# Group A's attention scores: keys without zero padding, two heads in the two row halves of the tensor engine

## The chip, the cores and the metric

The kernel runs on one core of one Trainium2 chip. A core has five engines that work from queues of their own, each in the order of its queue: TensorE (PE; its weight loads are listed as PEld), VectorE (DVE), ScalarE (ACT), GpSimd (POOL) and SyncE (SP, which here issues the loads). Matrix products read SBUF, the core's working memory of 128 partitions, and write PSUM, eight banks of 512 float32 columns on the same 128 partitions. The metric is device time in microseconds, lower is better.

## The reference

One decoder layer over 256 tokens of width 1024, in float32. Two groups of eight heads each attend side by side. Group A, which the change touches, has heads of 64:

```python
xn = rms_norm(h, norm_mix_g)
proj = jnp.einsum('bsd,de->bse', xn, w_in)
qa, ka, va, c_q, c_kv, k_rope = jnp.split(proj, cuts, axis=-1)
qa = rms_norm(qa.reshape(b, s, N_HEADS_A, HEAD_DIM_A), qnorm_a_g)
ka = rms_norm(ka.reshape(b, s, N_HEADS_A, HEAD_DIM_A), knorm_a_g)
...
out_a = dilated_attention(qa, ka, va, rel_bias).reshape(b, s, WIDTH_A)
...
mixed = jnp.concatenate([out_a, out_b], axis=-1)
h = h + jnp.einsum('bse,ed->bsd', mixed, w_o)
hn = rms_norm(h, norm_ffn_g)
hid = jnp.square(jax.nn.relu(jnp.einsum('bsd,df->bsf', hn, w_ff1)))
h = h + jnp.einsum('bsf,fd->bsd', hid, w_ff2)
```

dilated_attention is a causal softmax of q k / 8 plus a bias by distance, in which a key counts once for each of three dilated windows that reaches it. Group B is latent attention: its queries and keys come from the latents c_q and c_kv by a second projection.

## The kernel before

The 256 tokens are two tiles of 128. Large products run as three passes over operands that are split into a high and a low part (type float32r): ScalarE casts the high part (L215 for weights, L244 for activations), VectorE subtracts it (L216, L245). Weights come in chunks on the SP queue and are split piece by piece just ahead of their use. Small products (scores, mixed values, transposes) are plain float32.

Up to group B's attention the order of each queue is set by a scheduler, which interleaves the steps by its own estimate of their times; the order of the program and the number of buffers bound it. The steps of this part are: q and k of group A (projection, norm per head, transposition into qT_a and kT_a), group A's scores, the latents' projection (columns 384, 384 and 288 wide), group A's v (512 wide), the transposition and split of the latents (transposed_split: transposes of nats into a bank of the pool mm, then L244 and L245 into cT), and from there on group B's up-projections, first that of q (384 wide), for which an order is written out by hand.

qT_a holds a pair of heads on its 128 partitions: the even head on 0 to 63, the odd one on 64 to 127. kT_a has a block of 128 partitions for each head, filled with zeros by GpSimd (L344) and then with the head's keys in its own half (L378 on VectorE for the even heads, L379 on ScalarE for the odd ones). So the score product of a head contracts over all 128 partitions, and the other head's queries meet zeros.

UNITS divides the eight heads and two token tiles into six units of one PSUM bank each: for four heads at a time, the first tile's queries with 128 keys (four heads in a bank), and twice the second tile's queries with 256 keys (two heads in a bank). A unit goes through scores (PE into a bank of the pool sc, which has two), probs (VectorE adds the bias and finds the least, L402; ScalarE's exp, L405; VectorE's reciprocal and scaling, L406 and L408) and keys_first (four transposes into a bank of mm, which also has two, and a copy into pts, by VectorE for the first tile, L421, by ScalarE for the second, L423). Every matmul and transpose is issued on L144 or L147.

A function that the prediction reads as a pattern is values: it takes an even and an odd head in the two halves of the array's columns, 64 columns of weights each. In the trace these are the rows sc<-pts,va and mm<-pts,vb, with 128*64 as their rows and columns of the array.

## Time and profile before

| | |
|---|---|
| runs | 321.79, 322.65, 323.81 us; median 322.65 |
| profiled execution, span from first to last instruction | 320.9 us |
| PE busy, share of the span | 313.9 us, 98% |
| DVE, ACT, POOL busy | 204.9, 175.6, 38.4 us |
| granted TensorE clock, mean | 1.000 |

The profile gives the span of its execution alone; the runs' times hold what lies around a span as well. In a timeline a row begins with its start in microseconds from the span's begin and its length; neighbouring instructions of one kind are merged (x4). A matmul's length overlaps that of the next one, so the distance between starts tells what one costs in a stream. A plain float32 product shows as two records.

### The profile page before, as it was taken

To read this page: it belongs to the slowest core of one execution; us is meant where nothing else is said; L and a number is where in the kernel's file an instruction comes from. 1 tells how busy PE (TensorE), PEld (TensorE's weight loads), DVE (VectorE), ACT (ScalarE), POOL (GpSimd) and SP (SyncE) were. 2 spreads that over 40 slices of the span, in tenths; PEclk is the share of its full clock that TensorE was granted. 3 is DMA by queue.
4 is the path that set the end of the run, shared out by engine and by line. 5 is a ranking of instruction groups with operands and counts; after the bars stand their busy time and mean duration, and the time that the engine had idled before them with its cause. 6 is when DMAs were issued, how large, how long until landed. Compare 5 with 4: busy or idle time off the path is not lost.

```text
span 320.9 us, 4942 instructions
## 1 busy us (share of the span) xinstructions
PE 313.9 (98%) x1898; PEld 279.6 (87%) x1898; DVE 204.9 (64%) x384; ACT 175.6 (55%) x298; POOL 38.4 (12%) x61
## 2 busy tenths in 40 slices
PE   7999999999999999999999999999999999999995
PEld 4878999989986887899989989989889899899883
DVE  3769899955887993758774464654654745644632
ACT  5775568947785683448553553543633633535400
POOL 1025501180467000002000000000000000000000
PEclk9999999999999999999999999999999999999999
DMA  7989555153933263308655564646556564654002
GB/s 223 384 349 320 200 173 192 49 158 99 307 113 83 62 249 132 133 0 283 242 190 205 154 240 143 226 157 202 192 158 234 147 226 154 196 199 131 0 28 105
DMA packets 12296, 56.46 MB, mean 176 GB/s; under 512 B 1480, under 2 KB 3792, under 8 KB 7536
## 3 DMA queue, kind: packets, MB, share of 16 engines
q1 hardware_dynamic: 11072, 55.02, 50.3%
q10 hardware_dynamic: 1200, 1.12, 1.1%
q8 instruction: 15, 0.25, 0.3%
q14 instruction: 9, 0.07, 0.1%
HBM read 55.07 MB, written 1.06 MB: 175 GB/s over the span
## 4 chain that ended last, share of the span: by engine, by line
PE 96%; DMA 1%; ACT 1%; DVE 0%; issue 0%; DVEq 0%; SPq 0%; ACTq 0%
PE acc L144 58%; PE sc L144 19%; PE mm L144 15%; PE mm L147 4%; DMA big<-in_xt_dram 1%; ACT big L573 0%; ACT sqs L356 0%; ACT big L244 0%; ACT nats L593 0%; DVE x L706 0%; DVEq L759 0%; SPq L205 0%; ACT vb L597 0%; ACTq L244 0%
## 5 line engine op out<-in xcount | busy, mean ns | idle before, releaser
L144 PE MATMUL acc<-his,big 128*128 128x512 f32 (+2 forms) x576 | 176.2, 381 | 1.2 <-ACT big L244 1.2
L216 DVE TENSOR_TENSOR los<-raw,his 128x1024 fp32r<-128x1024 f32 (+3 forms) x106 | 121.5, 1149 | 85.9 <-ACT his L215 85.6
L215 ACT CAST his<-raw 128x1024 fp32r<-128x1024 f32 (+3 forms) x106 | 104.4, 992 | 100.5 <-PE acc L144 41.6
L144 PEld LDWEIGHTS acc<-his,big 128*128 128x128 f32 x576 | 107.4, 190 | 19.0 <-ACT big L244 1.9
L144 PE MATMUL acc<-los,big 128*128 128x512 f32 (+2 forms) x288 | 109.3, 380 | 0.0
L144 PEld LDWEIGHTS acc<-los,big 128*128 128x128 f32 x288 | 54.7, 190 | 8.6 <-issue 0.6
L144 PE MATMUL sc<-big,his 128*128 128x256 f32 x256 | 46.3, 283 | 0.0
L144 PE MATMUL mm<-big,his 128*128 128x256 f32 x256 | 46.2, 283 | 0.0
L144 PEld LDWEIGHTS sc<-big,his 128*128 128x128 f32 x256 | 40.2, 192 | 0.3
L144 PEld LDWEIGHTS mm<-big,his 128*128 128x128 f32 x256 | 40.1, 192 | 0.2
L144 PE MATMUL mm<-big,los 128*128 128x256 f32 x128 | 36.1, 283 | 0.0
L144 PE MATMUL sc<-big,los 128*128 128x256 f32 x128 | 36.0, 284 | 0.0
L144 PEld LDWEIGHTS mm<-big,los 128*128 128x128 f32 x128 | 24.5, 192 | 0.0
L144 PEld LDWEIGHTS sc<-big,los 128*128 128x128 f32 x128 | 24.5, 192 | 0.0
L405 ACT ACTIVATE half<-half,mx 128x128 f32<-128x128 f32 (+1 forms) x32 | 14.2, 445 | 4.4 <-DVE mx L402 4.2
L681 DVE TENSOR_TENSOR half<-half 128x512 f32<-128x512 f32 x16 | 10.9, 684 | 0.0
L684 DVE TENSOR_TENSOR big<-half,big 128x512 fp32r<-128x512 f32 x16 | 10.9, 684 | 0.0
L245 DVE SCALAR_TENSOR_TENSOR big<-mm,cols,big 128x256 fp32r<-128x256 f32 x16 | 7.3, 481 | 5.5 <-ACT big L244 5.2
L244 ACT ACTIVATE big<-mm,cols 128x256 fp32r<-128x256 f32 x16 | 7.3, 475 | 6.0 <-PE mm L147 5.8
L147 PE MATMUL mm<-ident,half 128*128 128x128 f32 x64 | 9.9, 273 | 0.0
L683 ACT CAST big<-half 128x512 fp32r<-128x512 f32 x16 | 9.7, 613 | 0.0
L147 PEld LDWEIGHTS mm<-ident,half 128*128 128x128 f32 x64 | 7.9, 140 | 1.5 <-DVE half L408 0.2
(129 smaller groups left out, 221.2 us busy)
## 6 DMA issues: line engine op xcount, KB each, us to landing
raw<-in_weights_dram SPq DMA_DIRECT2D x37, 1024.0 KB, 4.8
raw<-in_weights_dram SPq DMA_DIRECT2D x10, 512.0 KB, 3.6
raw<-in_weights_dram SPq DMA_DIRECT2D x6, 768.0 KB, 4.6
raw<-in_weights_dram SPq DMA_DIRECT2D x2, 576.0 KB, 4.1
raw<-in_weights_dram SPq DMA_DIRECT2D x4, 256.0 KB, 5.2
big<-in_xt_dram SPq DMA_DIRECT2D x4, 256.0 KB, 5.3
x<-in_x_dram SPq DMA_DIRECT2D x2, 512.0 KB, 8.5
big<-vec_d ACTq DMA_DIRECT2D x1, 1024.0 KB, 6.9
```

The costliest lines, as they stand in the source:

```text
L144: return self._issue(self.tc.nc.tensor.matmul(**kw))
L147: return self._issue(self.tc.nc.tensor.transpose(**kw))
L215: A.copy(out=hi, in_=raw)
L216: V.tensor_tensor(out=lo, in0=raw, in1=hi.bitcast(F32), op=ALU.subtract)
L244: a = A.activation(out=hi, in_=src, func=AF.Copy, scale=g)
L245: v = V.scalar_tensor_tensor(out=lo, in0=src, scalar=g, in1=hi.bitcast(F32), op0=ALU.mult, op1=ALU.subtract)
L405: A.activation(out=sb[:, i, :], in_=sb[:, i, :], func=AF.Exp, scale=-1.0, bias=mx[:, i:i + 1], accum_out=mx[:, 4 + i:5 + i])
L681: V.tensor_tensor(out=s2, in0=z, in1=z, op=ALU.mult)
L683: A.copy(out=ht[:, sl, :], in_=s3)
L684: V.tensor_tensor(out=ht[:, 4 + 2 * b:6 + 2 * b, :], in0=s3, in1=ht[:, sl, :].bitcast(F32), op=ALU.subtract)
```

## The change

kT_a becomes a tile of the shape of qT_a: a pair of heads on 128 partitions, no zeros and no fill, and one copy on VectorE in place of two. scores_a issues, for four heads and one token tile, four products of 64 rows each: the even head on partitions 0 to 63, the odd one on 64 to 127, in turn, the even heads into one bank and the odd ones into another. The bank is then a unit of two heads with every second head, so there are eight units; those of the first tile fill 256 columns of their bank, and have two transposes. probs and keys_first follow the unit's size. (The new file has its comments taken out, and its lines are numbered otherwise.)

```diff
-    kT_a = big.tile([P, H, S], F32, name="big")
-    G.memset(kT_a, 0.0)
+    kT_a = keep.tile([P, H // 2, S], F32, name="kT_a")
...
             else:
-                kv = kT_a.rearrange("p (h two) s -> p h two s", two=2)
-                V.tensor_copy(out=kv[0:64, :, 0, ts], in_=t3[0:64])
-                A.copy(out=kv[64:128, :, 1, ts], in_=t3[64:128])
...
+                V.tensor_copy(out=kT_a[:, :, ts], in_=t3)
...
-        sb = halft().rearrange("p (h k) -> p h k", h=n)
+        sb = halft(n * nk).rearrange("p (h k) -> p h k", h=n)
...
+        n, nk = sb.shape[1:]
+        blocks = n * nk // P
         flat = sb.rearrange("p h k -> p (h k)")
         ps = bank()
-        for i in range(4):
+        for i in range(blocks):
             T.transpose(out=ps[:, i * P:(i + 1) * P], in_=flat[:, i * P:(i + 1) * P], identity=ident)
         i = hs[0] - h0
+        dst = pT[:, i:i + (n - 1) * hs.step + 1:hs.step]
+        ps = ps[:, :blocks * P]
         if t == 0:
-            V.tensor_copy(out=pT[:, :, 0, :], in_=ps.rearrange("p (h s) -> p h s", h=4))
+            V.tensor_copy(out=dst[:, :, 0, :], in_=ps.rearrange("p (h s) -> p h s", h=n))
         else:
-            A.copy(out=pT[:, i:i + 2, 1:3, :], in_=ps.rearrange("p (h k s) -> p h k s", h=2, k=2))
+            A.copy(out=dst[:, :, 1:3, :], in_=ps.rearrange("p (h k s) -> p h k s", h=n, k=2))
...
-    for u in UNITS:
-        ps = scores(u, lambda h: qT_a[:, h // 2, :], lambda h: kT_a[:, h, :])
-        keys_first(u, probs(u, ps, lambda h: bias_r[:, h, ::-1], lambda t, h: -1.0), pT_a[u[0]])
...
+    def scores_a(h0):
...
+        for t in range(NT):
+            nk = (t + 1) * P
+            ps = [bank(sc).rearrange("p (h k) -> p h k", k=nk) for _ in range(2)]
+            for i in range(2):
+                for o in range(2):
+                    rs = slice(o * DA, (o + 1) * DA)
+                    T.matmul(out=ps[o][:, i, :], lhsT=qT_a[rs, h0 // 2 + i, t * P:(t + 1) * P], rhs=kT_a[rs, h0 // 2 + i, 0:nk], start=True, stop=True)
+            for o in range(2):
+                yield (h0, t, range(h0 + o, h0 + 4, 2)), ps[o][:, 0:2, :]
+
+    for h0 in (0, 4):
+        for u, ps in scores_a(h0):
+            keys_first(u, probs(u, ps, lambda h: bias_r[:, h, ::-1], lambda t, h: -1.0), pT_a[h0])
```

The scheduler orders the queues anew. On TensorE, the scores of the first four heads and the first tile stood like this, sc_396 being their one bank, with products of the latents' projection (acc) between them:

```order
L144 MATMUL sc_396<-big_207,qT_a_213 128x128
L144 MATMUL acc_618<-his_637,big_123 128x384
L144 MATMUL acc_618<-los_638,big_123 128x384
L144 MATMUL acc_618<-his_637,big_124 128x384
L144 MATMUL acc_617<-his_655,big_123 128x384
L144 MATMUL sc_396<-big_207,qT_a_213 128x128 x3
```

They stand like this now, sc_393 being the bank of the even heads and sc_394 that of the odd ones:

```order
L144 MATMUL acc_626<-his_646,big_124 128x384
L144 MATMUL sc_393<-kT_a_207,qT_a_212 128x128
L144 MATMUL sc_394<-kT_a_207,qT_a_212 128x128
L144 MATMUL sc_393<-kT_a_207,qT_a_212 128x128
L144 MATMUL sc_394<-kT_a_207,qT_a_212 128x128
```

The four products are together now, and the halves take turns; the same four heads' products of 256 columns stand in one such run of four a little later.

The scores of heads 4 to 7 are on TensorE further on. For the first tile sc_461 is the bank of the even heads and sc_462 that of the odd ones:

```order
L144 MATMUL acc_717<-his_736,big_124 128x288
L144 MATMUL sc_461<-kT_a_207,qT_a_212 128x128 x2
L144 MATMUL acc_716<-his_736,big_123 128x288
L144 MATMUL acc_716<-los_737,big_123 128x288
L144 MATMUL sc_462<-kT_a_207,qT_a_212 128x128 x2
L144 MATMUL acc_716<-his_736,big_124 128x288
```

For the second tile, sc_493 is the bank of the even heads and sc_494 that of the odd ones, and the transposes are those of two earlier units:

```order
L144 MATMUL acc_717<-his_770,big_123 128x288
L144 MATMUL sc_493<-kT_a_207,qT_a_212 128x256
L147 MATMUL mm_440<-ident_111,half_431 128x128 x4
L147 MATMUL mm_455<-ident_111,half_446 128x128 x4
L144 MATMUL sc_493<-kT_a_207,qT_a_212 128x256
L144 MATMUL sc_494<-kT_a_207,qT_a_212 128x256 x2
L144 MATMUL acc_717<-los_771,big_123 128x288
```

Here the products of one half stand together, apart from those of the other half, save for the second and third of the second tile.

On ScalarE, around the copies of group A's v out of its banks (va), the order was this; L423 copies the last two units' transposed probabilities, L244 makes the high parts of the transposed latents:

```order
L423 COPY pts<-mm 128x2x256
L215 CAST his<-raw 128x768
L423 COPY pts<-mm 128x2x256
L244 ACTIVATE big<-mm,cols 128x256
L215 CAST his<-raw 128x768
L244 ACTIVATE big<-mm,cols 128x256
L557 ACTIVATE va_209<-acc,rstd 128x512
L557 ACTIVATE va_210<-acc,rstd 128x512
L215 CAST his<-raw 128x768
L244 ACTIVATE big<-mm,cols 128x256 x2
```

It is this now, with L424 for L423 and L572 for L557:

```order
L424 COPY pts<-mm 128x2x256
L215 CAST his<-raw 128x768
L424 COPY pts<-mm 128x2x256
L572 ACTIVATE va_208<-acc,rstd 128x512
L572 ACTIVATE va_209<-acc,rstd 128x512
L215 CAST his<-raw 128x768
L244 ACTIVATE big<-mm,cols 128x256 x6
L215 CAST his<-raw 128x768
```

The two L244 that stood ahead of the copies of v are behind them and behind a cast. VectorE's L245 stand in a row of six in the same way, behind the low part of that cast. On TensorE the transposes of these latents, which were four ahead of v's last products and two behind them, are six behind them:

```order
L144 MATMUL acc<-his,big 128x512
L147 MATMUL mm<-ident,nats 128x128 x6
L144 MATMUL acc<-his,big 128x384
L144 MATMUL acc<-los,big 128x384
L144 MATMUL acc<-his,big 128x384 x2
```

## Rows read from the trace of the kernel before

**Rows 1.** The page: busy time (part 1) and chain of waits (part 4).

```profile
PE 313.9 (98%) x1898; PEld 279.6 (87%) x1898; DVE 204.9 (64%) x384; ACT 175.6 (55%) x298; POOL 38.4 (12%) x61
...
PE 96%; DMA 1%; ACT 1%; DVE 0%; issue 0%; DVEq 0%; SPq 0%; ACTq 0%
```

**Rows 2.** Busy time by stretch: us, PE, PEld, DVE, ACT, POOL, then PEclk, DMA.

```profile
40.00:50.00 10.00, 10.00 (x64) 9.86 (x63) 9.11 (x40) 6.74 (x20) 0.00 (x0) 1.00 0.64 214
50.00:60.00 10.00, 10.00 (x71) 9.66 (x70) 9.74 (x36) 8.67 (x26) 1.48 (x4) 1.00 0.30 99
```

**Rows 3.** Timeline of PE, 51.2 to 54.2 us: start, length, what.

```profile
51.45 1.69 PE L144 MATMUL sc<-big,qT_a 128*128 128x256 f32 x10
52.98 0.60 PE L147 MATMUL mm<-ident,half 128*128 128x128 f32 x4
53.42 0.39 PE L144 MATMUL sc<-big,qT_a 128*128 128x128 f32 x2
```

**Rows 4.** Timeline of PE, 124.2 to 126.5 us, at group B's mixed values.

```profile
124.04 0.39 PE L144 MATMUL acc<-los,big 128*128 128x512 f32 x1
124.26 0.40 PE L144 MATMUL acc<-his,big 128*128 128x512 f32 x1
124.59 1.52 PE L144 MATMUL mm<-pts,vb 128*64 128x256 f32 x16
126.04 0.50 PE L144 MATMUL acc<-his,big 128*128 128x512 f32 x1
126.38 0.40 PE L144 MATMUL acc<-los,big 128*128 128x512 f32 x1
```

**Rows 5.** Timeline of PE, 16.4 to 18.3 us, at the bias product.

```profile
16.26 0.84 PE L144 MATMUL acc<-his,big 128*128 128x512 f32 x3
17.03 0.81 PE L144 MATMUL sc<-big 32*8 32x384 f32 x2
17.77 0.50 PE L144 MATMUL acc<-los,big 128*128 128x512 f32 x1
```

**Rows 6.** Timeline of PE, 71 to 80 us, at the end of v's products.

```profile
74.97 0.39 PE L144 MATMUL acc<-his,big 128*128 128x512 f32 x1
75.20 0.38 PE L147 MATMUL mm<-ident,nats 128*128 128x128 f32 x2
75.34 0.42 PE L144 MATMUL acc<-his,big 128*128 128x384 f32 x1
75.60 0.34 PE L144 MATMUL acc<-los,big 128*128 128x384 f32 x1
75.78 0.52 PE L144 MATMUL acc<-his,big 128*128 128x384 f32 x2
```

**Rows 7.** Timeline of ACT, 71.5 to 80 us.

```profile
74.72 1.38 ACT L557 ACTIVATE va<-acc,rstd 128x512 f32<-128x512 f32 x2 [0.84 <-PE acc L144]
75.99 0.82 ACT L215 CAST his<-raw 128x768 fp32r<-128x768 f32 x1
76.71 0.47 ACT L244 ACTIVATE big<-mm,cols 128x256 fp32r<-128x256 f32 x1
```

**Rows 8.** Timeline of DVE, 72 to 80.5 us.

```profile
76.84 0.96 DVE L216 TENSOR_TENSOR los<-raw,his 128x768 fp32r<-128x768 f32 x1 [1.95 <-ACT his L215]
77.72 0.87 DVE L245 SCALAR_TENSOR_TENSOR big<-mm,cols,big 128x256 fp32r<-128x256 f32 x2
```

**Rows 9.** Waits: who waited for whom, us in total, times, longest.

```profile
PE acc L144 <- ACT big L244: 1.2, 1, 1.2
...
PE mm L147 <- ACT sqs L356: 0.5, 1, 0.5
```

**Rows 10.** Groups by form, 40 to 72 us: busy us, mean ns.

```profile
L144 PEld LDWEIGHTS sc<-big,qT_a 128*128 128x128 f32 x32 | 5.0, 190 | 0.2
...
L421 DVE COPY pts<-mm 128x512 f32<-128x512 f32 x2 | 1.4, 682 | 0.0
...
L379 ACT COPY big<-mm 64x512 f32<-64x512 f32 x2 | 1.2, 582 | 0.3 <-DVE big L378 0.3
```

## The prediction

> **What bounds the kernel now.** I read the page first. TensorE is busy 98% of the span, and the chain of waits is 96% TensorE [rows 1]: its instruction stream, taken in order, is the run. A change is worth what it adds to or takes from that stream, or the waits that it puts into it. The stretches between 40 and 60 us, where group A's scores run, show the same: PE is busy all of both, at a granted clock of 1.00 [rows 2]. VectorE is at 91 and 97% there, so I looked whether TensorE could come to wait for it.

> A row's duration overlaps the next row's, so I price a product by the distance between starts. Four transposes of 128 columns start at 52.98 and the next row at 53.42, which makes 0.11 us for one full-precision (fp32) pass of 128 columns. A score product is two such passes (the 16 products of the eight heads give 32 records, [rows 10]). The row at 51.45 holds ten passes, four of 256 columns and six of 128, and ends at 52.98: (1.53 - 0.66) / 4 = 0.217 us for a pass of 256 [rows 3]. So one head costs 2 x 0.11 + 2 x 0.217 = 0.654 us, and all eight cost **5.23 us**. That is all that the change can shrink.

> **The passes.** The diff keeps the number and the columns of the products. Each now uses 64 rows of the array, and two gain only if they run at once, which needs products of both halves next to each other. The order of the new program decides that. It has the scores in six bursts, each between other products: (1) four of 128 columns, halves alternating; (2) four of 256, alternating; (3) two of 128, both of the same half; (4) two of 128 of the other half; (5) one of 256, alone; (6) three of 256, of which the first two are of different halves. Whether halves overlap at all in fp32 no row of before shows for rows. The nearest is the mixed values, where an even and an odd head run in halves of the columns: sixteen passes, eight of 256 and eight of 128, would be 8 x 0.217 + 8 x 0.11 = 2.62 us one after the other, and the row takes 126.04 - 124.59 = 1.45 us [rows 4]. Two run at once. I take the same for rows. The bursts are then 0.44 + 0.87 + 0.44 + 0.44 + 0.43 + 0.87 = 3.49 us, **1.74 us less**; without any overlap they stay 5.23 us, no gain.

> **The ends of a burst.** The same rows give what it costs to go from the whole array to halves and back. The product ahead of the mixed values lasts 124.59 - 124.26 = 0.33 us where the one ahead of that lasts 0.22: 0.11 more. Inside, 1.45 against 2.62 / 2 = 1.31: 0.14. The product behind lasts 126.38 - 126.04 = 0.34: 0.12 [rows 4]. Together 0.37 for each of six bursts, **2.2 us more**. A second price is the bias product, which uses 32 rows: the three products ahead take 17.03 - 16.26 = 0.77 us instead of 0.66, its two passes of 384 columns take 0.74 instead of 2 x 0.325 [rows 5], and with 0.12 behind that is 0.32, or 1.9 us for six. The lower bound is nothing, if only column halves pay. I take 0.37 because those are heads in halves with two passes each, as here. Net of the passes and the ends: -1.74 + 2.2 = **+0.5 us** on TensorE.

> The loads of weights are hidden in before: one lasts 0.19 us, and passes over the same rows start 0.11 us apart [rows 3, 10]. I take that for passes of the same half as well.

> [...]

> **The wait before the latents' up-projection.** This term comes from what moved, not from the scores. Before, the first part of the transposed latents is split by ScalarE ahead of the copies of v (two L244 ahead of the two L557), and TensorE goes from v's last product at 74.97 over two transposes to the q projection at 75.34 without a gap [rows 6]. In the new order no L244 stands ahead of those copies. All six stand behind them and behind a cast of weights, and TensorE has six transposes between v's last product and the first q product, which needs the first L244.

> I count from the end of v's products, which is 75.20 in before. ScalarE starts the copies at 74.72 (the first bank is done earlier), the cast at 75.99, the L244 behind it at 76.71, and that ends at 76.71 + 0.47 = 77.18 [rows 7]. The sequence copy, copy, cast, L244 is the same now, so the first q product can start 2.0 us behind v's last. Six transposes cover 0.66 us. The wait is 2.0 - 0.66 = 1.35 us. Then two products run, 0.18 us each (75.78 - 75.60, [rows 6]), and the third needs the low part from VectorE's L245. VectorE has the same row as in before ahead of it, the low part of that cast: 76.84 to 77.72, and L245 itself takes half of 0.87 us and some, to 78.2 [rows 8]. 78.2 - 77.18 - 0.36 = 0.66 us more. Together **2.0 us**. Further on, a part is ready every 0.4 to 0.5 us and six products take 1.05 us, so nothing else is late. If one of the two were covered by something that I don't see, 0.7 or 1.35 us would be left.

> **The rest costs nothing while TensorE has cover.** ScalarE loses two copies of 0.58 us; GpSimd loses a fill that no row of TensorE waits for. VectorE gets eight units in place of six: two more reciprocals of a few columns, and four copies of 256 columns for two of 512 that took 0.68 us each. A copy of half the columns takes between 0.34 and 0.68 us, so the copies are 0 to 1.4 us more work, spread over 20 us [rows 10]. Followed through the new order with the durations of before, each unit's probabilities are ready over 1 us before TensorE comes to transpose them; if that cover went, VectorE's addition would show, some 1.4 us at most. The DMA queue keeps its order; its weight loads wait for VectorE's low parts, which come that much later at most, and TensorE takes a weight some microseconds after it has landed.

> **Sum.** +0.5 + 2.0 = +2.5 us. The profiled execution spans 320.9 us; the runs' median of 322.65 lies 1.7 us above that, and I put the sum on the median: **325.1 us**, 0.8% slower. About 1% is what a measurement of this kernel can tell from no change, so this counts as the same.

> **Rivals.**
> (a) Row halves don't run at once in fp32. The passes then save nothing and the ends and the wait stay: +2.2 + 2.0 = +4.2, 326.9 us, slower by 1.3%. It decides in bursts 1, 2 and 6: a burst 1 that takes 0.88 us in place of 0.44. For it: only column halves are seen to overlap; against it: those are the same kind of product.
> (b) Row halves cost nothing at their ends, and overlap in full: -1.74 + 2.0 = +0.3, 322.9 us. Against it stands the bias product [rows 5]. [...]
> (c) The wait of 2.0 us is paid back: TensorE waits later for ScalarE, 0.5 us before the transposed k and 1.2 us before the feed-forward part [rows 9], and ScalarE could get ahead during the pause. All of it back gives +0.8, 323.4 us. Against it: what ScalarE does there begins with TensorE's own later results.
> (d) Together, (b) and (c) give -1.4, 321.2 us; nothing that I see reaches 1% below.
> (e) Weight loads are not hidden behind passes of the same half: twelve such passes in bursts 3 to 6, 0.19 us each, +2.3 on the forecast, 327.4 us. The passes of [rows 3] speak against it. [...]

> **Chances.** Forecast 0.50 (324.3 to 326.0: 0.3 less by the bias product's ends, and 0.5 either way for the durations of the wait), (a) 0.16, (b) 0.14, (c) 0.11, (d) 0.03, (e) 0.03, something else 0.03. The range of 322.6 to 327.1 us takes in the forecast, (a), (b) and (c), with 0.2 to 0.3 us for the runs' spread, and leaves about 0.1 out; without (a), or without (b), more than 2 in 10 would be out. Slower by over 1% (above 325.9) are (a), (e) and a tenth of the forecast: 0.24. Faster by over 1% (below 319.4): 0.03. Within 1%: 0.73.

> **What would show it.** In the profile of the changed kernel: bursts 1 and 2 as rows of eight records whose next row starts 0.55 to 0.6 and 1.0 us later (twice the pass price if (a) holds); the product behind a burst at 0.10 us over its usual distance; bursts 3 and 4 at 0.58 us, dearer than two products of 128 columns in before (0.44 us); idle time of PE behind six transposes of the latents, released by L244 and then by L245 under their new line numbers, 1.3 and 0.7 us. The forecast is wrong if that idle time is missing, if TensorE waits for VectorE at the units' transposes, or if a burst's ends cost nothing.

## The result, and the profile after

The changed kernel took 326.2 us, the median of four executions (324.6, 325.2, 327.2 and one of 1,095 us, which is left out of the ratio; the median of the other three is 325.2 us), beside 322.6 us for the kernel before on the same chip. The ratio is 1.010, with a 95% interval of 1.0075 to 1.0124: 2.4 to 4.0 us slower, at the edge of what this kernel's measurement tells from no change. The forecast was 325.1 us.

The profiled execution spans 323.4 us, 2.5 more than before. That difference is not the change's alone. The first product of the latents (384 columns), ahead of which no product differs, starts at 29.14 us in before and at 28.82 us here; in the ten profiles of this study it starts between 28.2 and 30.4 us. I therefore measure the change on the **stretch** from that product to group A's first mixed values, which holds all that is changed. In before:

Timeline of PE of the kernel before: start, length, what.

```profile
29.14 0.42 PE L144 MATMUL acc<-his,big 128*128 128x384 f32 x1
...
91.94 0.44 PE L144 MATMUL sc<-pts,va 128*64 128x256 f32 x2
```

That is 62.80 us. The page of the changed kernel (parts 1 and 4), which answers to [rows 1]:

```profile
PE 314.7 (97%) x1898; PEld 277.8 (86%) x1898; DVE 205.3 (63%) x388; ACT 174.4 (54%) x296; POOL 34.7 (11%) x60
...
PE 95%; ACT 2%; DMA 1%; DVE 1%; issue 0%; DVEq 0%; SPq 0%; ACTq 0%
```

The chain now has 2% of ScalarE and 1% of VectorE in it: TensorE waits somewhere. The timeline of PE shows where, and bursts 1, 3 and 6 of the scores (the rows with kT_a); idle time before a row, and who ended it, stands in brackets:

```profile
28.82 0.42 PE L144 MATMUL acc<-his,big 128*128 128x384 f32 x1
...
44.21 0.33 PE L144 MATMUL acc<-los,big 128*128 128x384 f32 x1
44.39 0.34 PE L144 MATMUL acc<-his,big 128*128 128x384 f32 x1
44.66 0.71 PE L144 MATMUL sc<-kT_a,qT_a 64*128 64x128 f32 x8
45.30 0.45 PE L144 MATMUL acc<-his,big 128*128 128x384 f32 x1
45.58 0.34 PE L144 MATMUL acc<-los,big 128*128 128x384 f32 x1
...
54.28 0.71 PE L144 MATMUL sc<-kT_a,qT_a 64*128 64x128 f32 x4
54.92 0.41 PE L144 MATMUL acc<-his,big 128*128 128x288 f32 x1
...
60.52 1.14 PE L144 MATMUL sc<-kT_a,qT_a 64*128 64x256 f32 x6
...
74.87 0.39 PE L144 MATMUL acc<-his,big 128*128 128x512 f32 x1
75.10 0.82 PE L147 MATMUL mm<-ident,nats 128*128 128x128 f32 x6
77.14 0.44 PE L144 MATMUL acc<-his,big 128*128 128x384 f32 x1 [1.22 <-ACT big L244]
77.42 0.34 PE L144 MATMUL acc<-los,big 128*128 128x384 f32 x1
78.15 0.61 PE L144 MATMUL acc<-his,big 128*128 128x384 f32 x2 [0.39 <-DVE big L245]
...
94.40 0.44 PE L144 MATMUL sc<-pts,va 128*64 128x256 f32 x2
```

The stretch is 94.40 - 28.82 = 65.58 us, **2.78 us longer**. What follows it is not: from the mixed values to the end of the span it is 323.4 - 94.40 = 229.00 us here and 320.9 - 91.94 = 228.96 us in before.

Read the bursts first. Burst 1 has eight records (four products of two passes) and the next product starts 0.64 us behind its start; eight passes of 0.11 us one after the other would be 0.88. Burst 3 has half as many passes, all of one half, and takes the same 0.64 us. So the halves do run at once, and 0.2 us of each burst is no pass: four pass times of 0.11 us are 0.44. The product ahead of burst 1 lasts 44.66 - 44.39 = 0.27 us where the one ahead of that lasts 0.18, and the product behind it 45.58 - 45.30 = 0.28. A burst costs 0.1 ahead, 0.2 inside and 0.1 behind: 0.40 us.

Now the wait. Before, the q projection began 0.37 us behind the start of v's last product, over two transposes [rows 6]. Here it begins 77.14 - 74.87 = 2.27 us behind it, over six; four transposes are 0.44 us, so 1.46 us are waiting for L244. The third product waits for L245. The timelines of ACT and DVE show what stands ahead of these two, and answer to [rows 7, 8]:

```profile
74.67 1.31 ACT L572 ACTIVATE va<-acc,rstd 128x512 f32<-128x512 f32 x2 [0.86 <-PE acc L144]
75.88 0.82 ACT L215 CAST his<-raw 128x768 fp32r<-128x768 f32 x1
76.61 0.84 ACT L244 ACTIVATE big<-mm,cols 128x256 fp32r<-128x256 f32 x2
```

```profile
76.74 0.96 DVE L216 TENSOR_TENSOR los<-raw,his 128x768 fp32r<-128x768 f32 x1 [2.82 <-ACT his L215]
77.61 0.87 DVE L245 SCALAR_TENSOR_TENSOR big<-mm,cols,big 128x256 fp32r<-128x256 f32 x2
```

ScalarE takes the two copies of v (L572), a cast, and only then L244; VectorE takes the low part of that cast ahead of L245. It is the queue of the forecast, to 0.1 us. The list of waits has this wait as the second of two for L244; the first, 1.3 us, is at the start of the run, as the 1.2 us of [rows 9] are:

```profile
PE acc L144 <- ACT big L244: 2.6, 2, 1.3
...
PE mm L147 <- ACT sqs L355: 0.6, 1, 0.6
PE acc L144 <- DVE big L245: 0.4, 1, 0.4
```

### The profile page after: what moved, and what is told of

It is laid out like the page before. It is cut to its first block, busy times and chain, and to the rows that moved or that the text cites. A ratio compares the mean times of both kernels' runs of the same rounds, so it can differ in the third digit from the quotient of the medians.

```text
span 323.4 us, 4943 instructions
## 1 busy us (share of the span) xinstructions
PE 314.7 (97%) x1898; PEld 277.8 (86%) x1898; DVE 205.3 (63%) x388; ACT 174.4 (54%) x296; POOL 34.7 (11%) x60
## 4 chain that ended last, share of the span: by engine, by line
PE 95%; ACT 2%; DMA 1%; DVE 1%; issue 0%; DVEq 0%; SPq 0%; ACTq 0%
PE acc L144 57%; PE sc L144 19%; PE mm L144 15%; PE mm L147 4%; DMA big<-in_xt_dram 1%; ACT va L572 0%; ACT big L588 0%; DVE los L216 0%; ACT his L215 0%; ACT sqs L355 0%; ACT nats L608 0%; ACT big L244 0%; DVE x L721 0%; DVE big L245 0%; DVEq L774 0%
## 5 line engine op out<-in xcount | busy, mean ns | idle before, releaser
L244 ACT ACTIVATE big<-mm,cols 128x256 fp32r<-128x256 f32 x16 | 7.3, 478 | 7.5 <-PE mm L147 6.5
L245 DVE SCALAR_TENSOR_TENSOR big<-mm,cols,big 128x256 fp32r<-128x256 f32 x16 | 7.4, 483 | 4.8 <-ACT big L244 4.5
```

What stands on the lines that cost most here:

```text
L244: a = A.activation(out=hi, in_=src, func=AF.Copy, scale=g)
L245: v = V.scalar_tensor_tensor(out=lo, in0=src, scalar=g, in1=hi.bitcast(F32), op0=ALU.mult, op1=ALU.subtract)
```

## The experiments

The theory after this reading: two costs that add. The halves cost 0.65 us net (six pairs of ends at 0.40, less the passes saved), and 2.1 us is a wait that comes from the order of eight units, whatever the products are. Rivals: the wait belongs to the halves; the halves gain and the units cost more; ends are paid by product and not by burst; the waiting is paid somewhere in any order.

### Eight units, products over all rows

One part alone: the units, banks and transposes of the changed kernel, with padded keys and full products.

```diff
-    kT_a = keep.tile([P, H // 2, S], F32, name="kT_a")
+    kT_a = big.tile([P, H, S], F32, name="big")
+    G.memset(kT_a, 0.0)
...
-                V.tensor_copy(out=kT_a[:, :, ts], in_=t3)
+                kv = kT_a.rearrange("p (h two) s -> p h two s", two=2)
+                V.tensor_copy(out=kv[0:64, :, 0, ts], in_=t3[0:64])
+                A.copy(out=kv[64:128, :, 1, ts], in_=t3[64:128])
...
-                    T.matmul(out=ps[o][:, i, :], lhsT=qT_a[rs, h0 // 2 + i, ...], rhs=kT_a[rs, h0 // 2 + i, 0:nk], ...)
+                    T.matmul(out=ps[o][:, i, :], lhsT=qT_a[:, h0 // 2 + i, ...], rhs=kT_a[:, h0 + 2 * i + o, 0:nk], ...)
```

> One part alone: eight units of two heads and two banks as in the changed kernel, but the products as before, over all 128 rows with zero-padded keys. TensorE's queue has the same six bursts and the same place of the latents' transposes. Theory (the loss is a wait of 2.0 us that comes from the eight units' order, and +0.5 us that the row halves cost net of what they save): the wait is still there, released by L244 and then L245, 1.3 and 0.4 to 0.7 us; the scores cost 5.23 us and no ends; span 322.9 us, 2.0 above the kernel before and 0.5 below the changed one. Rival (the wait comes with the row halves, or the halves are the whole loss): no wait before the q projection, span 320.9 us. Rival (the halves gain 1.7 us and the units cost 4.2 us): span 325.1 us.

Measured: ratio 1.0103 (1.0076 to 1.0131), profiled span 324.3 us. Its timeline of PE:

```profile
30.39 0.42 PE L144 MATMUL acc<-his,big 128*128 128x384 f32 x1
...
78.06 0.44 PE L144 MATMUL acc<-his,big 128*128 128x384 f32 x1 [1.22 <-ACT big L244]
...
79.07 0.62 PE L144 MATMUL acc<-his,big 128*128 128x384 f32 x2 [0.39 <-DVE big L245]
...
95.32 0.44 PE L144 MATMUL sc<-pts,va 128*64 128x256 f32 x2
```

The wait is there to the hundredth, 1.22 and 0.39 us, without one product in a half: it belongs to the units. The stretch is 64.93 us, 2.13 above before and 0.65 below the changed kernel. The span says otherwise (3.4 above before, not the 2.0 expected) because its first latents' product starts 1.25 us later than before's. No score is on TensorE by then: its first wait, for the first L244 of the run, lasts 1.60 us here and 1.22 in before, and products of 512 columns start 0.43 us apart until 12.7 us, where in before they do so until 10.6 us and 0.23 us apart from then on. The runs, at 2.4 to 4.2 us above before, don't show the 0.65 us: this kernel's ratio equals the changed kernel's to 0.001. In four of its six executions, as in one of the changed kernel's three, the mean granted clock is 0.992 to 0.995 (0.997 to 1.000 in those of the kernel before), so they can hold time at the lower clock that the kept traces don't have; how much is open.

### The changed kernel, latents transposed early

The first latents' transposes get the scores' two banks, which are empty by then, in place of the pool that the last units' transposes hold.

```diff
-    def transposed_split(srcs, k0, n, g0, hi, lo):
+    def transposed_split(srcs, k0, n, g0, hi, lo, pool=None):
...
-            ps = bank()
+            ps = bank(pool or mm)
...
-        transposed_split([c[:, b * 384:] for c in cn], 3 * b, 3, G_C, *cT)
+        transposed_split([c[:, b * 384:] for c in cn], 3 * b, 3, G_C, *cT, pool=None if b else sc)
```

> The changed kernel, and the first latents' transposes go into the scores' two banks instead of the pool that the units' transposes use, so that they are not behind the last unit. TensorE takes them 17 products before the end of v's; the six bursts stay. Theory: the wait of 2.0 us is gone, since three of the L244 stand ahead of the copies of v; only the halves' +0.5 us is left, span 321.4 us, 2.0 below the changed kernel. Rival (the wait is paid somewhere else in any order, since ScalarE and VectorE have the same work): span 323.4 us, a new wait of 1 to 2 us at the q projection's later rows or at the transposed q.

Measured: ratio 1.0034 (1.0018 to 1.0049), span 321.4 us. Timeline of PE:

```profile
28.48 0.42 PE L144 MATMUL acc<-his,big 128*128 128x384 f32 x1
...
91.96 0.44 PE L144 MATMUL sc<-pts,va 128*64 128x256 f32 x2
```

The stretch is 63.48 us, 2.10 below the changed kernel: the wait is gone, and the six bursts are as they were. What is left above before is 0.68 us. Behind the mixed values this kernel is 0.44 us longer (321.4 - 91.96 = 229.44), so the rival has a fifth of its case: the first eight transposes of group B's q take 1.35 us (1.08 in the changed kernel), and the wait for its transposed k is 0.79 us for VectorE's scaling, in place of 0.55 us for ScalarE.

### Both, the fourth corner

The two edits above together; their core:

```diff
-            ps = bank()
+            ps = bank(pool or mm)
...
-                    T.matmul(out=ps[o][:, i, :], lhsT=qT_a[rs, h0 // 2 + i, ...], rhs=kT_a[rs, h0 // 2 + i, 0:nk], ...)
+                    T.matmul(out=ps[o][:, i, :], lhsT=qT_a[:, h0 // 2 + i, ...], rhs=kT_a[:, h0 + 2 * i + o, 0:nk], ...)
```

> The fourth corner: eight units with products over all rows and padded keys, and the first latents' transposes in the scores' banks. The stretch from the latents' first product (384 columns) to group A's mixed values was 62.80 us in the kernel before, 65.58 in the changed one, 64.93 with all rows and the wait, 63.48 with halves and the latents early. Theory (two costs that add: 2.1 us of wait from the eight units' order, 0.65 us net from the halves): 62.8 us, the kernel before's. Rival (the early transposes bring a gain of their own that hid a larger cost of the halves): below 62.5 us; rival (they bring a cost): above 63.1 us.

Measured: ratio 1.0015 (1.000 to 1.003), span 320.9 us. Timeline of PE:

```profile
28.61 0.42 PE L144 MATMUL acc<-his,big 128*128 128x384 f32 x1
...
91.46 0.44 PE L144 MATMUL sc<-pts,va 128*64 128x256 f32 x2
92.91 1.28 PE L147 MATMUL mm<-ident,nats 128*96 128x128 f32 x8
...
99.04 0.61 PE L147 MATMUL mm<-ident,nats 128*96 128x128 f32 x4 [0.77 <-DVE nats L617]
```

The stretch is 62.85 us, and the four corners are:

| stretch, us | latents where the change puts them | latents early |
|---|---|---|
| eight units, all rows | 64.93 | 62.85 |
| eight units, halves | 65.58 | 63.48 |

Across, 2.08 and 2.10 us; down, 0.65 and 0.63 us; and the corner with neither is at before's 62.80. The two costs add, and eight units in place of six cost TensorE nothing by themselves. With the early latents come some 0.45 us behind the stretch: here the first transposes of q take 1.28 us in place of 1.08, and the wait for the transposed k is 0.77 us in place of 0.55.

### The halves one after the other

```diff
-            for i in range(2):
-                for o in range(2):
+            for o in range(2):
+                for i in range(2):
```

> The changed kernel with the two products of one half before the two of the other, in place of alternating ones; units, banks and the number of bursts stay. Theory (halves run at once only where a product of the other half comes right behind): of eight passes in bursts 1 and 2 only the two at the change of half overlap, so 7 in place of 4 pass times: 0.77 in place of 0.44 us and 1.52 in place of 0.87 us, and 0.2 us in the last three products: +1.2 us, span 324.6 us (+1.7 us if none overlap). Rival (the pairs of records that start 0.007 us apart are no overlap, and the short bursts come from something else): bursts as long as in the changed kernel, span 323.4 us.

Measured: ratio 1.0083 (1.0058 to 1.0108), span 323.8 us, and a stretch of 94.83 - 29.25 = 65.58 us, the changed kernel's to the hundredth. Timeline of PE at bursts 1 and 2:

```profile
45.08 0.72 PE L144 MATMUL sc<-kT_a,qT_a 64*128 64x128 f32 x8
45.73 0.45 PE L144 MATMUL acc<-his,big 128*128 128x384 f32 x1
...
50.27 1.14 PE L144 MATMUL sc<-kT_a,qT_a 64*128 64x256 f32 x8
51.35 0.44 PE L144 MATMUL acc<-los,big 128*128 128x384 f32 x1
```

My theory falls: alternating is not what makes the halves overlap. With two products of one half queued ahead of two of the other, the bursts take 0.65 and 1.08 us, as before the edit. They do overlap, though, and the rival is wrong in that: by the single starts in the trace the eight records still come in four pairs, now 0.013 to 0.014 us apart where alternating gave 0.006 to 0.007. The products of the second half start while a pass of the first half, queued ahead of them, has not begun.

### Each product twice

```diff
+                    for _ in range(2):
                         T.matmul(out=ps[o][:, i, :], ...)
```

on top of the last edit; the second product gives the first one's result again.

> The changed kernel with each score product issued twice (the second gives the same result again), first all of one half, then all of the other. Burst 1 is then four products of one half ahead of four of the other, 16 records; the others are bursts of four products of one half. Theory (the halves' queues run independently, as seen where two products of one half stood ahead of two of the other, and a burst has one entry and one exit): burst 1 takes 0.65 + 4 x 0.11 = 1.09 us, bursts of four 128-column products of one half 0.64 + 4 x 0.11 = 1.08 us. Rival (TensorE looks only two products ahead): burst 1 takes some 1.3 to 1.5 us. Rival (the price is per product, not per burst): 1.3 us in both kinds.

One execution: 330.7 us. Timeline of PE:

```profile
44.01 1.71 PE L144 MATMUL sc<-kT_a,qT_a 64*128 64x128 f32 x16
45.65 0.44 PE L144 MATMUL acc<-his,big 128*128 128x384 f32 x1
...
55.80 1.16 PE L144 MATMUL sc<-kT_a,qT_a 64*128 64x128 f32 x8
56.89 0.65 PE L147 MATMUL mm<-ident,half 128*128 128x128 f32 x4
```

Four products of one half in a row take 56.89 - 55.80 = 1.09 us, as the theory of the ends said: 0.45 for two products more, and no further ends. Burst 1, four of one half ahead of four of the other, takes 1.64 us and not 1.09. In the trace its first four records start 0.11 us apart, alone; then come three pairs, 0.004 to 0.006 us apart, with a single behind the first of them, and five singles: 13 pass times in place of 8. The other half's first product starts with the third of the first half (the record beside that one lasts 0.37 us, as only the first record of a half does; the others last 0.27), so TensorE reached about two products ahead. That is the rival, somewhat beyond its range.

### The ends alone

Only the second query tile's scores use halves; the first tile's use all rows of padded keys, in units of four heads as before.

```diff
...
+        ps = bank(sc).rearrange("p (h k) -> p h k", k=P)
+        for i in range(4):
+            T.matmul(out=ps[:, i, :], lhsT=qT_a[:, (h0 + i) // 2, 0:P], rhs=kP_a[:, h0 + i, :], start=True, stop=True)
+        yield (h0, 0, range(h0, h0 + 4)), ps
...
```

> Only the scores of the second query tile use halves of the rows, from keys without padding; the first query tile's use all rows of padded keys, with units of four heads as before. The four pairs of 256-column products then stand in four bursts, each of one half alone, so that no pass can be saved, and the latents' transposes stand where the kernel before has them. Theory (each burst costs 0.40 us at its ends whether or not halves run at once; the wait comes from the eight units): four ends, no wait, 62.8 + 1.6 = 64.4 us from the latents' first product to group A's mixed values, each burst about 0.2 us ahead and behind dearer than four passes of 0.217 us. Rival (only a change from half to half costs, or alternating does): 62.8 us. Rival (the wait comes with the halves): 66.5 us.

Measured: ratio 1.0061 (1.0049 to 1.0073), span 322.5 us. Timeline of PE:

```profile
29.07 0.42 PE L144 MATMUL acc<-his,big 128*128 128x384 f32 x1
...
47.37 1.13 PE L144 MATMUL sc<-kT_a,qT_a 64*128 64x256 f32 x4
48.42 0.44 PE L144 MATMUL acc<-his,big 128*128 128x384 f32 x1
...
93.47 0.44 PE L144 MATMUL sc<-pts,va 128*64 128x256 f32 x2
```

The stretch is 64.40 us: 1.60 more than before for four bursts that save nothing and with no wait at the latents, so 0.40 us a burst. Its four passes of 0.217 us take 48.42 - 47.37 = 1.05 us.

### Whole bursts

Each four products in program order, the first into the bank that comes free last, so that a burst isn't broken.

```diff
+            T.in_order = True
             for i in range(2):
-                for o in range(2):
+                for o in (1, 0):
...
+            T.in_order = False
```

> The changed kernel with each four score products kept together, the first into the bank that comes free last: four bursts in place of six, all alternating. Theory of the ends (0.40 us for each burst, besides its passes): passes 2.62 in place of 3.49 us and two ends fewer, together -1.7 us in the scores. But the last burst comes 37 products later, so the last unit's probabilities do; with the wait before the q projection as it is, span 321.7 us. Rival (both banks have to be free before a burst, so VectorE stands still during it and its later units come too late): TensorE waits for VectorE at the last units' transposes or for ScalarE's L244 longer, 1 to 3 us, span 322.7 to 324.7 us. Rival (ends are paid per product and not per burst): the scores stay within 0.9 us of the changed kernel's, span 322.5 us.

Measured: ratio 1.0155 (1.0126 to 1.0184), span 324.8 us. Timeline of PE:

```profile
28.34 0.42 PE L144 MATMUL acc<-his,big 128*128 128x384 f32 x1
...
69.75 1.13 PE L144 MATMUL sc<-kT_a,qT_a 64*128 64x256 f32 x8
...
74.04 0.63 PE L147 MATMUL mm<-ident,half 128*128 128x128 f32 x4 [1.80 <-DVE half L405]
76.33 0.41 PE L147 MATMUL mm<-ident,half 128*128 128x128 f32 x2 [1.66 <-DVE half L405]
...
79.74 0.52 PE L144 MATMUL acc<-los,big 128*128 128x384 f32 x1
80.06 0.64 PE L144 MATMUL acc<-his,big 128*128 128x384 f32 x2
...
95.80 0.44 PE L144 MATMUL sc<-pts,va 128*64 128x256 f32 x2
```

Four bursts, all paired, take 3.42 us from start to next start by the single starts in the trace (the six took 4.68), and two entries and two exits fewer, 0.1 us each outside the bursts, bring the saving to the 1.7 us expected. The stretch is 67.46 us all the same, 1.9 above the changed kernel: the last burst starts at 69.75 us (60.52 in the changed kernel), and TensorE stands 1.80 and 1.66 us for the probabilities of the last units. The first rival holds, but its waits are not the whole loss: 3.46 us in place of the changed kernel's 2.1, less the 1.7 saved, would leave the stretch 0.3 us shorter. The rest is mostly TensorE's clock. Busy time by stretch (us, PE, PEld, DVE, ACT, POOL, then PEclk, DMA):

```profile
75.00:80.00 5.00, 3.54 (x15) 3.04 (x16) 2.49 (x7) 3.02 (x9) 0.00 (x0) 0.69 0.33 105
```

Behind the two waits the granted clock was 0.50 from 76.9 to 80.3 us, and a product of 384 columns took 80.06 - 79.74 = 0.32 us there, where it takes 0.18 at 1.00 [rows 6]. Work that filled 3.4 us at 0.50 would fill some 1.7 at 1.00, an estimate from these two prices. In the changed kernel's trace the clock stays at 1.00 through its wait, so its 2.78 us hold nothing of this.

### One whole burst in the kernel before

Where both score banks are empty anyway, at the start, a burst needn't be broken. The kernel before, with the first four heads' 256-column products first and in halves, and the early latents.

```diff
+    kU_a = keep.tile([P, 2, S], F32, name="kU_a")
...
+    first = [bank(sc).rearrange("p (h k) -> p h k", k=S) for _ in range(2)]
+    for i in range(2):
+        for o in range(2):
+            rs = slice(o * DA, (o + 1) * DA)
+            T.matmul(out=first[o][:, i, :], lhsT=qT_a[rs, i, P:S], rhs=kU_a[rs, i, :], start=True, stop=True)
...
```

> The kernel before (padded keys, all rows, units of four heads for the first query tile and for the last four heads' second tile), but the first four heads' 256-column products come first, from unpadded keys in halves of the rows, while both score banks are empty anyway, so that they stand in one whole burst; and the first latents' transposes go into the scores' banks. Theory: one burst saves four passes of 0.217 us (0.87 us) and pays one pair of ends (0.40 us), a gain of 0.45 us, and there is no wait ahead of the q projection: 62.4 us from the latents' first product to group A's mixed values against 62.8 in the kernel before and in the kernel with eight units and early latents; behind that the early latents cost 0.4 to 0.5 us as they did there, so that nothing is left of it in the whole time (ratio 1.000, within 0.3%). Rival (a whole burst gains nothing, its ends cost 0.9 us): 62.8 us. Rival (keys of both tiles are needed sooner, or the units come later): a wait of 0.5 to 2 us of TensorE in the stretch, 63 to 65 us.

Measured: ratio 0.9991 (0.9973 to 1.0008), span 320.1 us. Timeline of PE:

```profile
28.66 0.42 PE L144 MATMUL acc<-his,big 128*128 128x384 f32 x1
...
91.08 0.44 PE L144 MATMUL sc<-pts,va 128*64 128x256 f32 x2
```

The stretch is 62.42 us, 0.38 below before: four passes saved, one pair of ends paid. Behind it nothing is lost here (320.1 - 91.08 = 229.02), where I had expected the early latents' 0.4 us, so that loss does not come with the early latents in every order. In the runs it is not to be told from the kernel before.

## Why the prediction was right, point by point

**The passes.** Right, -1.74 us: the net of 0.65 us, from the corners, less six ends of 0.40 us leaves 1.75 us. The reason given, that products of both halves must stand next to each other, was right in the sense of within two products, not of alternating: with four of a half ahead of four of the other, burst 1 of the doubled kernel took 13 pass times in place of 8.

**The ends.** Right in kind, a little small: 0.37 us a burst from column halves [rows 4], 0.40 us measured for row halves. With six bursts 2.2 became 2.4 us, so the net was 0.65 and not 0.5 us. The bursts inside were dearer than column halves' (0.2 against 0.14 us), hence 0.64 us for bursts 3 and 4 where I expected 0.58. Over all rows there is no such price: two transposes and the product behind them take 75.60 - 75.20 = 0.40 us [rows 6], which is two passes of 0.11 us and a product of 0.18. With the halves one after the other, TensorE did not start every pass in the order of its queue, which I had given for all five engines. That is how I read the four pairs: the record doesn't name the half, but passes of one half start 0.11 us apart, so the one 0.013 us behind is of a product that stands two further back.

**The wait.** Right: 2.0 forecast, 2.1 us measured by the corners, 1.46 us for L244 (1.35 forecast) and, by the third product's start 78.15 - 77.14 = 1.01 us behind the first's in place of 0.44 [rows 6], 0.57 us for L245 (0.66 forecast; 0.39 us of it is listed as idle time). That it comes from the units' order and not from the scores is now shown and not argued.

**What costs nothing.** Right: eight units cost the stretch 0.05 us, and TensorE never waits for VectorE at the units' transposes. VectorE's copies of 256 columns took 0.42 us each, where I had left 0.34 to 0.68 open. The cover hangs on where the bursts stand: with whole bursts, the last of them 9 us later, TensorE waits for exactly that, 1.80 and 1.66 us.

**The rivals.** (a) and (b) fall with the bursts, (d) with (b), and (e) with burst 3, where passes of the same half follow at 0.11 us. (c) falls, since what follows the stretch is the same to 0.04 us; and of its two waits I had misplaced one: the 1.2 us stand at the start of the run, not ahead of the feed-forward part.

**The sum.** 2.78 us in the trace against 2.5; the runs' 2.4 to 4.0 us hold both.

## What to carry to other kernels

Two halves of the rows at once are worth it when a stay in halves saves more than its 0.40 us: by these prices four fp32 products of 128 columns just break even (0.44 us saved), four of 256 gain some 0.4 us (0.38 in the run with one whole burst), and a burst of one half only loses (0.40 us each in the run of the ends alone). The banks that let VectorE work ahead are the same that break the bursts: kept whole in the changed kernel, the bursts brought waits of 1.80 and 1.66 us, and where both banks were empty anyway the whole burst came without one. And look at what a new division into units does to the queues behind it: here the loss was three quarters a wait at another stage, found by following one engine's queue, and gone by giving one set of transposes other banks.
